# A batched matrix product: one TensorE loop over all 32 batches, the first pair of x loaded in fp32, the last pair's output copied over all partitions

## The chip, the cores and the metric

The kernel runs on one core of one Trainium2 chip. The metric is the device time of one execution in microseconds (us). The engines are TensorE (PE; its weight loads are listed apart as PEld), VectorE (DVE), ScalarE (ACT), GpSimd (POOL) and SyncE (SP). SP and POOL issue the transfers between DRAM and the on-chip memory here; these all run on the core's 16 DMA engines. TensorE writes to PSUM, and DVE and ACT copy from there to SBUF.

## The reference

```python
batch, m, k, n = 32, 512, 1024, 768
x = randn(batch, m, k)        # float32
weight = randn(batch, k, n)   # float32
out = np.matmul(x, weight).astype(np.float32)
```

There are 32 independent products of a 512x1024 matrix with a 1024x768 matrix. Inputs and output are fp32 in DRAM. x is 2.10 MB a batch, weight 3.15 MB and out 1.57 MB.

## The kernel before

**Precision and layout.** The products run in bf16. POOL's DMAs cast while they load: `load_w(b)` brings the weights of batch b into one of four slots `ws` (L92), and `load_x(k)` brings the x of two batches into one of two slots `xs` (L101). Such a pair slot holds the one batch in partitions 0 to 63 and the other in 64 to 127, eight rows of x to a partition. TensorE needs x with k on the partitions, so `transpose` (L153) turns it by multiplying with an identity: the bf16 pairs are taken as fp32 words, one 128x128 block of words in each of 32 transposes per pair, in eight groups of four. DVE copies each group from PSUM (`pts`) to `both` (`spread_pair`, L233). `multiply(b, mt)` (L134) then makes one of four row blocks of a batch: eight steps over k, each with two matmuls (512 and 256 columns) into the PSUM banks `pms`. Two blocks share three banks.

**The batches before.** Batch 0 is alone. SP loads its x in fp32 (L359) into `x_first`, which lies in an output slot; TensorE transposes fp32 numbers, and `spread_first` casts them (L216). Batches 1 to 30 go in pairs (1,2), (3,4), and so on; batch 31 is alone again, with an x load of half the size (L99) and its own `spread_last` (L236). On TensorE, `on_pe` has the code of batch 0, then a loop of seven turns (L191) with two pairs in each, then the code of one more pair and of batch 31. All other engines have their instructions written out. At the end of a turn TensorE lowers the semaphores that count the copies, so that the same constants serve in each turn.

**Outputs.** ACT and DVE copy the banks to an output slot (L265, L268, L279, L281). A slot of `outs` holds batches (0,1), (2,3) and so on, batch 2a in partitions 0 to 63 and 2a+1 in the rest, and is stored with one DMA of 3.15 MB (`store`, L109). The last two batches are copied over all 128 partitions (L276): batch 30 to a tile of its own, `one`, batch 31 to a slot of `outs`. They are stored in halves by SP (`store_half`, L115). `slot_free` waits until a slot's earlier store has landed.

**Order of the transfers.** POOL's list (`on_pool`) sets it by hand: w0, x of pair 0, w1, w2, x of pair 1, and w3 go without any wait; then, in each odd batch, the x of the pair after the next (after the transposes of two pairs earlier, `pt_done`), the store of an earlier output pair, and a w (after the products of four batches earlier, `mm_done`); in each even batch a w. Three stores (11 to 13) are kept until after the last w. SP waits for each w in turn and passes a flag to TensorE (`landed`, L307, semaphore `s_wr`); ACT does the same for x (`s_xr`). TensorE takes these flags in `take` (L157). SP then issues the half of batch 30, store(14), and the other three halves.

Of the kernel before, what the change touches and what calls it, by code (L numbers as in the profile page):

```python
# [12 lines left out]
def kernel(  # L13
# [16 lines left out]
    AHEAD = 3  # L30
    LATE = 4
    HELD = 4
    GROUPS = 2 * MT
    W_SLOTS, X_SLOTS, OUT_SLOTS = 4, 2, 4
    LOOPS = (B - 4) // W_SLOTS
    LOOPED = 2 * LOOPS

# [3 lines left out]
    x_view = x.rearrange("b (mi mo) k -> b mi mo k", mi=P)  # L41
    pair_view = x[1:B - 1].rearrange("(p r) (mi mo) k -> p (r mi) mo k", r=2, mo=2 * MT)
    out_view = out.rearrange("b (mi mo) n -> b mi (mo n)", mi=P)
# [9 lines left out]
    outs = [sbuf(f"out{i}", [P, 2 * ROW], F32) for i in range(OUT_SLOTS)]  # L53
    one = sbuf("one", [P, ROW], F32)
    x_first = outs[3][:, :MT * K].rearrange("p (mo k) -> p mo k", mo=MT)
# [11 lines left out]
    s_first, s_zero, s_ident = sem("s_first"), sem("s_zero"), sem("s_ident")  # L67
# [13 lines left out]
    def pt_done(k):  # L81
        return GROUPS * (k + 2)

    def out_done(b):
        return 2 * (b + 1)
# [8 lines left out]
    def load_x(k):  # L94
        if k >= X_SLOTS:
            pool.wait_ge(s_pt, pt_done(k - X_SLOTS))
        slot = xs[k % X_SLOTS]
        if 2 * k + 1 == B - 1:
            pool.dma_start(out=slot[:, :MT], in_=x_view[B - 1]).then_inc(s_x[k % X_SLOTS], 16)  # L99
        else:  # L100
            pool.dma_start(out=slot, in_=pair_view[k]).then_inc(s_x[k % X_SLOTS], 16)  # L101
# [5 lines left out]
    def store(eng, a, sem):  # L107
        copied(eng, out_done(2 * a + 1) - 1)
        eng.dma_start(out=two_view[a], in_=outs[a % OUT_SLOTS]).then_inc(sem, 16)  # L109

    def store_half(b, p):
        src = one if b == B - 2 else outs[(b // 2) % OUT_SLOTS]
        half = slice(p * N2, (p + 1) * N2)
        copied(sp, 2 * b + p)
        sp.dma_start(out=out_view[b, :, half], in_=src[:, half]).then_inc(s_fin, 16)  # L115
# [3 lines left out]
    def stationary(b, mt):  # L119
        if b == 0 or b == B - 1:  # L120
            return both[mt][:, 0].rearrange("p j h i r -> p j (h i) r")
        return both[mt][:, (b - 1) % 2].rearrange("p j h i r -> p j (h i) r")
# [20 lines left out]
    def rows_of(b, g):  # L143

        if b == 0:
            return [x_first[:, g // 2, JT * (g % 2) + i::KT] for i in range(JT)]
        words = xs[(b // 2) % X_SLOTS].bitcast(F32)
        mo = g if b == B - 1 else g // 2 + MT * (g % 2)
        return [words[:, mo, j::JT] for j in range(JT)]

    def transpose(b, g):
        for i, rows in enumerate(rows_of(b, g)):
            last = pe.transpose(pts[g % 2][:, i, :], rows, ident)  # L153
        last.then_inc(s_pt, 1)
# [4 lines left out]
    def pair_on_pe(k, q):  # L159

        b = 2 * k + 1
        take(s_xr)
        for g in range(GROUPS):
            if GROUPS * q + g > 1:
                pe.wait_ge(s_c, GROUPS * q + g - 1)
            transpose(b, g)
        for r in range(2):
            take(s_wr)
            for mt in range(MT):
                at = 4 * q + 2 * r + mt // 2  # L170
                if not r:
                    pe.wait_ge(s_c, GROUPS * q + 2 * mt + 2)
                pe.wait_ge(s_a, at + 1 + mt % 2)
                if b + r == B - 2 and mt == MT - 1:
                    pe.wait_ge(s_dp, 2 * (B - 2))
                else:
                    pe.wait_ge(s_d, at + 1 + mt % 2)
                multiply(b + r, mt)

    def on_pe():  # L180
        pe.wait_ge(s_ident, 1)
        pe.wait_ge(s_first, 16)
        for g in range(GROUPS):
            if g > 1:
                pe.wait_ge(s_c, g - 1)
            transpose(0, g)
        pe.wait_ge(s_c, GROUPS).then_inc(s_c, -GROUPS)
        take(s_wr)
        for mt in range(MT):
            multiply(0, mt)  # L190
        with pe.Fori(0, LOOPS):  # L191
            for q in range(2):
                pair_on_pe(q, q)
            pe.wait_ge(s_c, 2 * GROUPS).then_inc(s_c, -2 * GROUPS)
            pe.wait_ge(s_a, 9).then_inc(s_a, -8)
            pe.wait_ge(s_d, 9).then_inc(s_d, -8)
        pair_on_pe(LOOPED, 0)
        b = B - 1
        take(s_xr)
        for g in range(MT):  # L200
            pe.wait_ge(s_c, GROUPS + max(g - 1, 0))
            transpose(b, g)
        take(s_wr)
        for mt in range(MT):
            j = 2 * b + mt // 2
            pe.wait_ge(s_c, GROUPS + mt + 1)
            pe.wait_ge(s_ap if mt % 2 else s_a, j - 1 if mt % 2 else 5 + mt // 2)
            pe.wait_ge(s_dp, j - 1)
            multiply(b, mt)
# [3 lines left out]
    def spread_first(g):  # L213
        xT, pt = both[g // 2][:, 0].rearrange("p j h i r -> p j (h i) r"), pts[g % 2]
        for j in range(2):
            last = dve.tensor_copy(  # L216
                xT[:, 2 * (g % 2) + j].rearrange("p (h i) r -> p r h i", h=2),
                pt[:, 2 * j:2 * j + 2].rearrange("p r (i h) -> p r h i", h=2),
            )
        return last  # L220

    def spread_pair(k, g):

        pt = pts[g % 2].bitcast(BF16).rearrange("p j (b i r) -> p j b i r", b=2, r=2)
        tile, half = both[g // 2], g % 2
        if 2 * k + 2 == B - 2:

            rows = tile[:, 1].rearrange("p j h i r -> p j (h i r)").rearrange(
                "p j (m r) -> p j m r", r=2
            )  # L230
            dve.tensor_copy(tile[:, 0, :, half], pt[:, :, 0])  # L231
            return dve.tensor_copy(rows[:, :, half::2, :], pt[:, :, 1])  # L232
        return dve.tensor_copy(tile[:, :, :, half].rearrange("p b j i r -> p j b i r"), pt)  # L233

    def spread_last(g):
        return dve.tensor_copy(  # L236
            both[g][:, 0].rearrange("p j h i r -> p (j h i r)"),
            pts[g % 2].bitcast(BF16).rearrange("p j m -> p (j m)"),
        )

    def slot_free(eng, b):
        a = b // 2
        if a >= OUT_SLOTS and b % 2 == 0 and b < B - 2:
            eng.wait_ge(s_st[a % OUT_SLOTS], 16 * (a // OUT_SLOTS))
        if b == B - 1:
            eng.wait_ge(s_st[a % OUT_SLOTS], 16 * (a // OUT_SLOTS))

    def pieces(b, p, i):

        pm = pms[p][i]  # L250
        if b >= B - 2:
            dst = one if b == B - 2 else outs[(b // 2) % OUT_SLOTS]
            at = p * N2 + 512 * i
            return [(dst[:, at:at + 512], pm)]
        mine = outs[(b // 2) % OUT_SLOTS][H * (b % 2):H * (b % 2 + 1)]
        starts = [p * N2 + h * ROW + 512 * i for h in range(2)]
        return [(mine[:, at:at + 512], pm[H * h:H * (h + 1)]) for h, at in enumerate(starts)]

    def out_on_act(b, p):
        j = 2 * b + p  # L260
        if p == 0:
            slot_free(act, b)
# [7 lines left out]
    def out_on_dve(b, p):  # L270
        j = 2 * b + p
        if p == 0:
            slot_free(dve, b)
        dve.wait_ge(s_mm, 2 * j + 2)
        if b >= B - 2:
            dve.tensor_copy(*pieces(b, p, 1)[0]).then_inc(s_dp, 1)  # L276
            return
# [4 lines left out]

    def on_dve():

        for b in range(B):
            if b == 0 or b % 2:
                spread = {0: spread_first, B - 1: spread_last}.get(b)
                for g in range(MT if b == B - 1 else GROUPS):
                    dve.wait_ge(s_pt, (0 if b == 0 else pt_done(b // 2 - 1)) + g + 1)
                    (spread(g) if spread else spread_pair(b // 2, g)).then_inc(s_c, 1)  # L290
                if b:
                    out_on_dve(b - 1, 1)
            out_on_dve(b, 0)
            if b % 2 or b == B - 1:
                out_on_dve(b, 1)

    def on_act():
        for b in range(B):
            out_on_act(b, 0)
            if b % 2 == 0:  # L300
                landed(act, (s_x, s_xr), b // 2)
            out_on_act(b, 1)

    def landed(eng, what, i):

        slots, ready = what
        eng.wait_ge(slots[i % len(slots)], 16 * (i // len(slots) + 1)).then_inc(ready, 1)  # L307

    def on_pool():
# [12 lines left out]
        load_x(0)  # L322
        load_w(1)
        load_w(2)
        load_x(1)
        for b in range(B):
            if b % 2 and b + AHEAD + 1 < B:
                load_x((b + AHEAD) // 2)
            a = (b - 5) // 2
            if b % 2 and 0 <= a < B // 2 - 1 - HELD:  # L330
                store(pool, a, s_st[a % OUT_SLOTS])
            if b + AHEAD < B:
                load_w(b + AHEAD)
            if b == B - LATE:
                for a in range(B // 2 - 1 - HELD, B // 2 - 2):
# [60 lines left out]
```

## Time and profile before

| | us |
|---|---|
| median of 3 runs | 513.71 (513.47 to 514.14) |
| the profiled execution | 514.01 |
| its span, from the first instruction to the last | 512.2 |
| TensorE's first matmul starts at | 12.41 |
| last matmul group starts at, and takes | 490.72, 10.56 |
| last store is issued at, and lands after | 502.09, 9.0 |

| engine | busy, us | share |
|---|---|---|
| PE | 437.9 | 85% |
| DVE | 206.8 | 40% |
| ACT | 110.2 | 22% |
| POOL | 33.7 | 7% |

Busy times are those of instructions that work on data; waiting and issuing DMAs are not counted. The slices of the page cut the span into 40 parts of 12.8 us, with a digit for the busy tenths of each. The GB/s of the DMA rows and windows count what is written at the destination; a load that casts fp32 to bf16 reads twice that from DRAM. Both the span and the two times around it are needed later: the profiled execution took 1.8 us more than its span, and 0.3 us more than the median.

### The profile page before, as it was taken

What the parts mean: (1) busy time and instruction counts of PE and PEld (TensorE: products, weight loads), DVE (VectorE), ACT (ScalarE), POOL (GpSimd) and SP (SyncE); (2) the same over time, 40 slices, a digit from 0 to 9 for tenths busy, and PEclk for the clock granted to TensorE, in tenths of its full rate; (3) what the DMA queues carried; (4) which work ended last, traced back from release to release, by engine and by line L of the source; (5) the groups of instructions that cost most, each with busy time, mean ns of one, the idle gap of its engine ahead of it and who ended that gap; (6) DMA issues with size and microseconds to landing.
All of it is one profiled execution on the core that took longest, in us unless ns stands there. A gap on an engine that the chain in (4) does not pass through costs nothing. (4 is left out here: it accounts for less than half of the span.)

```text
span 512.2 us, 6109 instructions
## 1 busy us (share of the span) xinstructions
PE 437.9 (85%) x2576; PEld 278.8 (54%) x2576; DVE 206.8 (40%) x332; ACT 110.2 (22%) x189; POOL 33.7 (7%) x68
## 2 busy tenths in 40 slices
PE   0899989999795997979989798898969979799991
PEld 0666656666463654636646365464635646456660
DVE  0463543545362352533525245153631615416230
ACT  1013122222211221112221122112122121221210
POOL 3000000101010010100101001010100100100000
PEclk9999999999997998979989899799998989979997
DMA  8999999999999999999999999999999999999996
GB/s 254 214 214 222 222 207 224 213 225 325 220 335 218 240 312 224 333 218 255 297 222 337 218 264 286 219 339 218 288 266 213 341 216 306 250 214 257 432 429 290
DMA packets 9803, 135.40 MB, mean 264 GB/s; under 512 B 1088, under 2 KB 1088, under 8 KB 1600
## 3 DMA queue, kind: packets, MB, share of 16 engines
q0 software_dynamic: 8928, 126.88, 96.3%
q1 hardware_dynamic: 864, 8.39, 4.0%
q8 instruction: 5, 0.08, 0.1%
q14 instruction: 6, 0.05, 0.0%
HBM read 167.77 MB, written 50.33 MB: 426 GB/s over the span
## 5 line engine op out<-in xcount | busy, mean ns | idle before, releaser
L134 PE MATMUL pm<-w,xT 128*128 128x256 bf16 (+1 forms) x2048 | 356.2, 337 | 40.2 <-PEq L157 40.2
L134 PEld LDWEIGHTS pm<-w,xT 128*128 128x128 bf16 x2048 | 205.8, 101 | 186.2 <-issue 61.5
L279 DVE COPY out<-pm 64x512 f32<-64x512 f32 x120 | 82.5, 687 | 198.9 <-PE pm L134 198.1
L265 ACT COPY out<-pm 64x512 f32<-64x512 f32 (+1 forms) x122 | 70.7, 580 | 292.8 <-PE pm L134 292.1
L233 DVE COPY xT<-pt 128x1024 bf16<-128x1024 bf16 x112 | 72.2, 687 | 61.0 <-PE pt L153 61.0
L153 PE MATMUL pt<-ident,x 128*128 128x128 f32 x496 | 80.0, 302 | 10.5 <-DVE xT L233 9.5
L153 PEld LDWEIGHTS pt<-ident,x 128*128 128x128 f32 x496 | 69.2, 209 | 21.8 <-DVE xT L233 17.4
L268 ACT COPY out<-pm 64x512 f32<-64x512 f32 (+1 forms) x62 | 35.8, 578 | 90.0 <-PE pm L134 90.0
L281 DVE COPY out<-pm 64x512 f32<-64x512 f32 x60 | 41.2, 686 | 0.0
L101 POOL DMA_DIRECT2D x<-in_x_dram x15 | 8.0, 532 | 266.6 <-PE pt L153 266.4
L92 POOL DMA_DIRECT2D w<-in_weight_dram x32 | 17.2, 538 | 125.4 <-PE pm L134 124.4
L153 PE MATMUL pt<-ident,out 128*128 128x128 f32 x32 | 6.9, 373 | 12.7 <-DMA out<-in_x_dram 12.4
L153 PEld LDWEIGHTS pt<-ident,out 128*128 128x128 f32 x32 | 5.3, 207 | 14.1 <-issue 12.4
L216 DVE CAST xT<-pt 128x256 bf16<-128x256 f32 x16 | 6.0, 441 | 14.4 <-PE pt L153 14.1
L109 POOL DMA_DIRECT2D out_dram<-out x14 | 7.5, 536 | 1.2 <-DVE out L281 0.7
L231 DVE COPY xT<-pt 128x512 bf16<-128x512 bf16 x8 | 3.4, 420 | 4.1 <-PE pt L153 4.1
L276 DVE COPY out<-pm 128x512 f32<-128x512 f32 x2 | 1.4, 692 | 8.4 <-PE pm L134 8.4
L236 DVE COPY xT<-pt 128x1024 bf16<-128x1024 bf16 x4 | 2.6, 688 | 5.2 <-PE pt L153 5.2
L232 DVE COPY xT<-pt 128x512 bf16<-128x512 bf16 x8 | 3.3, 416 | 0.0
L276 DVE COPY one<-pm 128x512 f32<-128x512 f32 x2 | 1.4, 687 | 3.2 <-PE pm L134 3.2
L265 ACT COPY one<-pm 128x512 f32<-128x512 f32 x2 | 1.2, 585 | 4.0 <-PE pm L134 4.0
L268 ACT COPY one<-pm 128x512 f32<-128x512 f32 x2 | 1.2, 586 | 4.0 <-PE pm L134 4.0
(8 smaller groups left out, 2.7 us busy)
## 6 DMA issues: line engine op xcount, KB each, us to landing
w<-in_weight_dram POOLq DMA_DIRECT2D x32, 1536.0 KB, 41.6
out_dram<-out POOLq DMA_DIRECT2D x14, 3072.0 KB, 36.9
x<-in_x_dram POOLq DMA_DIRECT2D x15, 2048.0 KB, 30.0
out_dram<-out SPq DMA_DIRECT2D x1, 3072.0 KB, 19.9
out<-in_x_dram SPq DMA_DIRECT2D x1, 2048.0 KB, 11.3
out_dram<-one SPq DMA_DIRECT2D x2, 768.0 KB, 13.4
out_dram<-out SPq DMA_DIRECT2D x2, 768.0 KB, 10.0
x<-in_x_dram POOLq DMA_DIRECT2D x1, 1024.0 KB, 25.3
```

Of the source, the lines that this page charges most:

```text
L92: pool.dma_start(out=ws[b % W_SLOTS], in_=w_view[b]).then_inc(s_w[b % W_SLOTS], 16)
L101: pool.dma_start(out=slot, in_=pair_view[k]).then_inc(s_x[k % X_SLOTS], 16)
L109: eng.dma_start(out=two_view[a], in_=outs[a % OUT_SLOTS]).then_inc(sem, 16)
L134: last = pe.matmul(pm[bank][:, at:at + size], xT[:, ko // 2, :, ko % 2], w[:, ko, off:off + size], start=(ko == 0), stop=(ko == KT - 1),)
L153: last = pe.transpose(pts[g % 2][:, i, :], rows, ident)
L216: last = dve.tensor_copy(xT[:, 2 * (g % 2) + j].rearrange("p (h i) r -> p r h i", h=2), pt[:, 2 * j:2 * j + 2].rearrange("p r (i h) -> p r ...
L231: dve.tensor_copy(tile[:, 0, :, half], pt[:, :, 0])
L233: return dve.tensor_copy(tile[:, :, :, half].rearrange("p b j i r -> p j b i r"), pt)
L265: last = act.copy(*piece)
L268: act.copy(*pieces(b, p, 2)[0]).then_inc(s_ap, 1)
L279: last = dve.tensor_copy(*piece)
L281: dve.tensor_copy(*pieces(b, p, 2)[1]).then_inc(s_dp, 1)
```

## The change

Pairs now begin at batch 0, (0,1) to (30,31), so that the pairs of x and of the output are the same ones.

- TensorE: one loop of eight turns, two pairs in each, holds all 32 batches. Nothing stands before or after it but the wait for the identity. The closing branch is marked with a hint. Semaphores are lowered by the last wait of a turn that needs them (`await_copies`) instead of by waits of their own; ACT and DVE raise `s_a` and `s_d` by two at the start.
- The first pair's x: SP loads all of it, 4.19 MB in fp32, to the space of output slots 2 and 3. DVE casts four of its eight rows per partition into `xs[0]`, ACT the other four (`cast_first`). ACT's last cast waits for DVE's and raises `s_xr`. TensorE's transposes are the same as for every pair.
- Load order: w0, w1, x of pair 1, w2, w3; then per pair an x, a store and two w. Two stores (12, 13) are kept until after the last w instead of three.
- The last pair: batch 30 and batch 31 share one output slot, each over all 128 partitions, copied in pieces of 64 partitions each; the tile `one` is gone. `spread` makes two DVE copies a group there. SP issues store(14) ahead of the four halves.

```diff
-    LOOPS = (B - 4) // W_SLOTS
-    LOOPED = 2 * LOOPS
+    LOOPS = B // W_SLOTS
...
-    pair_view = x[1:B - 1].rearrange("(p r) (mi mo) k -> p (r mi) mo k", r=2, mo=2 * MT)
+    x_view = x.rearrange("(p r) (mi mo) k -> p (r mi) mo k", r=2, mo=2 * MT)
...
+    x_first = all_outs[:, 4 * ROW:4 * ROW + 2 * MT * K].rearrange("p (mo k) -> p mo k", mo=2 * MT)
...
     def pt_done(k):
-        return GROUPS * (k + 2)
+        return GROUPS * (k + 1)
+    def last_out(b):
+        return outs[(PAIRS - 1) % OUT_SLOTS][:, ROW * (b % 2):ROW * (b % 2 + 1)]
...
+    def await_copies(s, n, last, step):
+        wait = pe.wait_ge(s, n)
+        if n == last:
+            wait.then_inc(s, -step)
...
+    def pair_on_pe(k):
         take(s_xr)
         for g in range(GROUPS):
+            if GROUPS * k + g > 1:
+                pe.wait_ge(s_c, GROUPS * k + g - 1)
+            transpose(k, g)
+        for b in (2 * k, 2 * k + 1):
             take(s_wr)
             for mt in range(MT):
+                if b % 2 == 0:
+                    await_copies(s_c, GROUPS * k + 2 * mt + 2, 2 * GROUPS, 2 * GROUPS)
+                at = 2 * b + mt // 2 + 1 + mt % 2
+                await_copies(s_a, at, 9, 8)
+                await_copies(s_d, at, 9, 8)
+                multiply(b, mt)
     def on_pe():
         pe.wait_ge(s_ident, 1)
...
-        with pe.Fori(0, LOOPS):
-            for q in range(2):
-                pair_on_pe(q, q)
...
+        with nc.Fori(0, LOOPS, engines=[mybir.EngineType.PE], hint_back_edge=True):
+            for k in range(2):
+                pair_on_pe(k)
...
+    def spread(k, g):
         pt = pts[g % 2].bitcast(BF16).rearrange("p j (b i r) -> p j b i r", b=2, r=2)
+        if k == PAIRS - 1:
+            for b in range(2):
+                rows = both[g // 2][:, b].rearrange("p j h i r -> p j (h i r)")
+                rows = rows.rearrange("p j (m r) -> p j m r", r=2)[:, :, g % 2::2, :]
+                last = dve.tensor_copy(rows, pt[:, :, b])
+            return last
+        return dve.tensor_copy(both[g // 2][:, :, :, g % 2].rearrange("p b j i r -> p j b i r"), pt)
...
         if b >= B - 2:
-            return [(dst[:, at:at + 512], pm)]
+            return [(last_out(b)[half, at:at + 512], pm[half]) for half in rows]
...
+    def cast_first(eng, copy, rows):
+        eng.wait_ge(s_first, 16)
+        for mo in rows:
+            if mo == 2 * MT - 1:
+                eng.wait_ge(s_cast, 1)
+            last = copy(xs[0][:, mo], x_first[:, mo])
+        return last
     def on_dve():
+        dve.sem_inc(s_d, 2)
+        cast_first(dve, dve.tensor_copy, range(MT)).then_inc(s_cast, 1)
...
     def on_act():
+        act.sem_inc(s_a, 2)
+        cast_first(act, act.copy, range(MT, 2 * MT)).then_inc(s_xr, 1)
         for b in range(B):
             out_on_act(b, 0)
-            if b % 2 == 0:
-                landed(act, (s_x, s_xr), b // 2)
+            if b % 2 and b < B - 1:
+                landed(act, s_x, s_xr, b // 2 + 1, (b // 2 + 2) // 2)
             out_on_act(b, 1)
...
-        load_x(0)
         load_w(1)
+        load_x(1)
         load_w(2)
-        load_x(1)
...
+        load_w(3)
+        for k in range(PAIRS - 2):
+            load_x(k + 2)
+            if k >= 2:
+                store(pool, k - 2, s_st[(k - 2) % OUT_SLOTS])
+            load_w(2 * k + 4)
+            load_w(2 * k + 5)
+        for a in range(PAIRS - 2 - HELD, PAIRS - 2):
+            store(pool, a, s_st[a % OUT_SLOTS])
...
-        store_half(B - 2, 0)
-        store(sp, B // 2 - 2, s_fin)
-        store_half(B - 2, 1)
-        store_half(B - 1, 0)
-        store_half(B - 1, 1)
+        store(sp, PAIRS - 2, s_fin)
+        for b in (B - 2, B - 1):
+            for p in range(2):
+                store_half(b, p)
```

## The prediction

> **What bounds the kernel now.** I read the page's head, slices and byte counts first, to see which resource has no idle time.
>
> ```profile
> span 512.2 us, 6109 instructions
> ...
> PE 437.9 (85%) x2576; PEld 278.8 (54%) x2576; DVE 206.8 (40%) x332; ACT 110.2 (22%) x189; POOL 33.7 (7%) x68
> ...
> DMA  8999999999999999999999999999999999999996
> ...
> HBM read 167.77 MB, written 50.33 MB: 426 GB/s over the span
> ```
>
> The DMA row has a 9 in all slices but the first and the last; no compute engine is near that. Second, the windows by stage (the columns after the granted clock are DMA share and GB/s as written; loads halve fp32 to bf16, so 218 written is 436 read).
>
> ```profile
> 0.00:2.00 2.00, 0.00 (x0) 0.00 (x0) 0.00 (x0) 1.09 (x1) 0.73 (x5) 1.00 0.09 25
> 2.00:12.40 10.40, 0.00 (x0) 0.02 (x1) 0.00 (x0) 0.19 (x1) 3.33 (x8) 1.00 1.01 295
> 31.00:115.00 84.00, 80.06 (x499) 52.77 (x497) 41.07 (x64) 21.42 (x37) 5.28 (x10) 1.00 1.02 218
> ...
> 482.00:508.00 26.00, 18.98 (x119) 11.98 (x117) 5.26 (x8) 4.10 (x7) 0.00 (x0) 0.94 0.99 421
> 508.00:511.00 3.00, 0.00 (x0) 0.00 (x0) 0.00 (x0) 0.00 (x0) 0.00 (x0) 0.50 0.22 92
> 511.00:512.20 1.20, 0.00 (x0) 0.00 (x0) 0.00 (x0) 0.00 (x0) 0.00 (x0) 0.50 0.00 0
> ```
>
> Loads run at 436 GB/s, stores at 421. So 167.77 MB / 436 = 384.8 us and 50.33 MB / 421 = 119.5 us: 504.3 us of transfers. With 2.0 us ahead of the first one and 1.2 us after the last, 507.5 of the 512.2 us are explained. The other 4.7 us are the ramp at the start and the last 3 us, where 92 GB/s say that only a few of the 16 DMA engines are still working: they finish unevenly. Third, the waits:
>
> ```profile
> POOL x L101 <- PE pt L153: 266.4, 13, 31.4
> POOL w L92 <- PE pm L134: 124.4, 14, 9.3
> PE pm L134 <- PEq L157: 40.2, 13, 5.2
> ```
>
> TensorE waits 40.2 us for weights (L157 takes the flag that SP passes on after a landing). POOL waits for TensorE to free buffers, but that does not starve the queue: in the issue table a w takes 41.6 us from issue to landing, of which its own 3.15 MB are 7.2 us, so it stands about 34 us behind others. The timeline shows why: a pair of batches that waits for nothing takes TensorE 112.02 - 85.56 = 26.46 us (5.66 us of transposes, 20.8 of products); its transfers take 9.6 (x) + 14.4 (w) + 7.5 (out) = 31.5 us. TensorE has 5.0 us to spare in every pair.
>
> **The change part by part.** Bytes: the same 167.77 and 50.33 MB of DRAM. What moves is the *first* transfers, the order of a few, and TensorE's code.
>
> First x: SP now loads 4.19 MB in fp32 instead of 2.10, and the pool queue loads 2.10 MB less with a cast. SP still issues it first (0.95 us, first packets at 2.0), so the start of the DMA does not move. Rate bounds for the moved 2.10 MB: 389 GB/s in 4 to 6 us, where nearly all was SP's fp32, costs 2.10 x (1/389 - 1/436) = +0.6 us; no difference costs 0. The nearest steady row of fp32 transfers, 427 GB/s in 494 to 501 us, gives 2.10 x (1/427 - 1/436) = +0.1. I take +0.1.
>
> TensorE's start: now at 12.41 us. In the DMA view 80 SP packets of 16 KB and 2 of POOL's start from 1.2 to 6.0 us, so 5 on each engine; after that SP and POOL share. The remaining 48 of 128 (0.79 MB) took until 12.3 us: 125 GB/s. Afterwards 4.19 - 1.31 = 2.88 MB remain, 23 us at that rate, landing at 29; alone it would land at 2.0 + 9.6 = 11.6. Rows are now 32 KB long and SP's 24 KB rows go as one packet, so its share should grow; I take 21. Then the casts, four 128x1024 on DVE and four on ACT. The nearest rows, 128x1024 bf16 at 687 ns and 64x512 f32 at 687 (DVE) and 580 (ACT), bound DVE by 4 x 0.69 = 2.7 and 8 x 0.69 = 5.5, ACT by 8 x 0.58 = 4.6 (scaled by elements); ACT's last waits for DVE's four, so 2.7 to 5.5 + 1.2 = 6.7. I take 4.6: TensorE starts at about 26 us, between 14 and 36.
>
> Is that on the path? Only if the queue runs dry. The queue holds SP's x (9.6), w0 to w3 (28.8) and x1 (9.6) without any wait: work until 50.0 us. TensorE finds w0 and w1 there (9.6 + 14.4 us of transfers, 26 us). Then in order x2 until 59.6, w4 66.8, w5 74.0, x3 83.6, w6 90.8, w7 98.0. The tightest is w7: load_w(7) waits for batch 3's products, two pairs after the start, T0 + 52.9, + 0.5 for the issue, + at most 4.3 us to the first packet (POOL's first issue at 1.48, packets at 5.8). 90.8 - 57.7 gives T0 < 33.1. With T0 = 26, 7 us of cover remain. The others (w5 35.5, x4 34.6, x2 39.5) are looser, and from store(0) on each pair brings 31.5 us of transfers against 26.5 of compute. So the late start costs 0; without the cover it is one us per us.
>
> The DVE casts are fp32 from SBUF to SBUF. [...]
>
> One loop: prologue (32 transposes, 64 products), two pairs, and an epilogue become two pairs. A turn closes with a branch:
>
> ```profile
> L191 PEldq COMPARE_BRANCH  x7: 76/208/228, 83.2 to 459.0; - x7
> ```
>
> One branch more, plus a hint of unknown cost: between 0 and, for a missed 16 KB of code, 5.2 us (the longest idle of TensorE that the waits show) per turn. TensorE's 2 x 5.0 us of slack in a turn cover both ends. [...] The row has 0.2 us a branch, for a body of 640 instructions (320 matmuls, each with its weight load), and the instruction queue q8 fetches nothing from 80 to 460 us. [...] Code: q8 fetched 5 blocks (0.08 MB), two of them after 460; half the code needs two or three less. Each occupies one DMA engine by 16 KB, 0.6 us at 436/16 GB/s; it helps only if that engine is the last: 0 to -0.6, taken -0.1.
>
> The end: POOL keeps two stores (6.3 MB, 14.9 us) instead of three behind the last weights, SP the same five (3.15 + 4 x 0.79 MB, 14.9 us). The last store was issued at 502.09 and landed 9.0 us later, at 511.1 (issue rows). If that end holds, the last w lands near 511.1 - 29.8 = 481; then batch 31's 10.4 us (13.3 where the granted clock fell, at 448 us): products end by 492 to 495, against 501.3 now. The last pair's copies over halves of the partitions are twice as many: after the last product DVE has 3 x 0.69 = 2.1 us instead of 0.7, and SP issues the last half at about 495 to 498 instead of 502.09. At 498 the queue still has 13 us of work, 1.9 of them its own. Cover 11 us; it hid 7 us before. Cost 0. `spread` in the last pair takes 2 x 0.42 instead of 0.69 eight times, 1.2 us, under the same cover. The x of the other pairs is asked for at pt_done(k) as before, with tens of us of queue ahead of it. SP's list of weight landings is unchanged, and its stores still stand behind the last of them.
>
> Sum: 512.2 + 0.1 - 0.1 = 512.2 us of span. The profiled execution took 514.01, 1.8 around its span, and the median of the runs is 0.3 below it: 513.7 for the median afterwards.
>
> New waits: DVE and ACT wait for SP's x before anything else, and behind them stand only the spreads and copies that need TensorE's first results; ACT's last cast waits for DVE's four, priced above. ACT's wait for the next pair's landing moves from the middle of batch 2k to the middle of 2k+1; behind it are that batch's remaining copies, and TensorE at that point needs the same x. SP issues store(14) ahead of the halves of batch 30, which stand behind its wait; pair 14's copies are done a batch earlier, so that wait is none. POOL issues w1 ahead of x1, 7 us of queue in the right direction for batch 1. The last pair's copies wait in slot_free for store(11), which now stands ahead of w30 in the queue and so has landed before batch 30 can start. Each costs 0.
>
> **The rivals.** (1) Slower: the queue runs dry once, at w7 near 91 us. Place: POOL's wait in load_w. Decides from T0 = 33. For it: SP got only 125 GB/s beside POOL, and 29 + 6.7 = 36; price 36 - 33.1 = 3 us, 517. Against: the long rows, and a first-packet delay of 4.3 us that falls in the busy start. (2) Slower: the hint makes each closing branch fetch a block, 7 x 0.6 = 4.2 us on one engine; if that one is among the last, 516 to 518. Against: q8 is silent in the loop now. (3) Faster: the uneven finish shrinks, since less code is fetched late and the products end some 6 us earlier. Half of the 3 us at 92 GB/s: 512.2. Against: the stores were never waited for at the end. (4) The change does not do what it says: the hint does nothing visible; that is my forecast's time.
>
> **How the numbers follow.** Forecast (no idle DMA, same bytes): 0.70, with its own range 512.8 to 514.6. Rival 1: 0.08, rival 2: 0.06, something slower that no row shows: 0.04; rival 3: 0.12. A measurement of this kernel can tell about 0.2%, 1.0 us, from no change. So slower 0.18, faster 0.12. The range 512.5 to 515.6 takes in the unpriced ends (+0.6, -0.6 and the runs' own 0.7 us) and the near parts of rivals 1 and 3.
>
> **What would show it.** Right: DMA digits of 9 throughout, 426 GB/s, TensorE's first transposes at 22 to 30 us, its waits at the landing flag still there (5 us a pair, less early on), last product near 493, the last store issued over 8 us before the end. Wrong: a slice with a lower DMA share between 50 and 120 us (rival 1), more than 5 packets on q8 (rival 2), a last stretch shorter than 2 us (rival 3), or total DMA rate below 424 GB/s without any gap.

## The result and the profile after

The changed kernel takes 514.36 us (median, 513.72 to 515.04), the kernel before 513.38 on the same chip (512.94 to 514.14): a ratio of 1.0017, 95% interval 1.0011 to 1.0024. It is slower by 1.0 us. The 513.71 us of the front page was a high reading of the kernel before, and so was its profiled execution (514.01): in the five comparisons of this document its median was 513.34 to 513.63. Ratios below are against the kernel before in the same comparison, "+0.98" is the difference of those medians.

The page of the changed kernel (an execution of 514.2 us):

```profile
span 512.4 us, 6044 instructions
...
PE 429.7 (84%) x2512; PEld 277.5 (54%) x2560; DVE 212.9 (42%) x332; ACT 116.4 (23%) x197; POOL 33.2 (6%) x67
...
DMA  8999999999999999999999999999999999999996
...
q8 instruction: 1, 0.02, 0.0%
HBM read 167.77 MB, written 50.33 MB: 426 GB/s over the span
```

The row of 9s, the bytes and the 426 GB/s are those of before. TensorE's work is off the path as before, and what the change moved lies where the prediction put it. Three answers show it: TensorE's waits (us in total, times, longest), the casts of the first pair (busy, mean ns, idle before), and the last rows of the timeline:

```profile
PE pm L125 <- PEq L143: 26.7, 8, 5.3
PE pt L139 <- PEq L143: 22.8, 1, 22.8
```

```profile
L231 DVE CAST x<-outs 128x1024 bf16<-128x1024 f32 x4 | 2.5, 689 | 18.7 <-DMA outs<-in_x_dram 18.7
L231 ACT CAST x<-outs 128x1024 bf16<-128x1024 f32 x4 | 3.9, 1042 | 16.5 <-DMA outs<-in_x_dram 16.5
```

```profile
497.78 1.39 DVE L221 COPY outs<-pm 64x512 f32<-64x512 f32 x2 [3.20 <-PE pm L125]
499.09 0.69 DVE L223 COPY outs<-pm 64x512 f32<-64x512 f32 x1
499.85 0.33 SPq L108 DMA_DIRECT2D out_dram<-outs  x1
```

SP's x lands at 18.7 us, TensorE starts at 22.8, still waits for weights at the landing flag (L143), and the last half-store is issued at 499.85, 11.4 us ahead of its landing. None of these places shows a stall of the queue.

That leaves the start, the finish and what lies around the span, and it is in the last two. The last microseconds, DMA share and GB/s in the last two columns; first the kernel before in the run b_again (513.43 us), which is nearer to its median than the profile of the front page, then the changed kernel:

```profile
507.00:508.00 1.00, 0.00 (x0) 0.00 (x0) 0.00 (x0) 0.00 (x0) 0.00 (x0) 0.50 0.74 307
508.00:509.00 1.00, 0.00 (x0) 0.00 (x0) 0.00 (x0) 0.00 (x0) 0.00 (x0) 0.50 0.37 154
509.00:510.00 1.00, 0.00 (x0) 0.00 (x0) 0.00 (x0) 0.00 (x0) 0.00 (x0) 0.50 0.18 74
510.00:511.00 1.00, 0.00 (x0) 0.00 (x0) 0.00 (x0) 0.00 (x0) 0.00 (x0) 0.50 0.00 0
```

```profile
507.00:508.00 1.00, 0.00 (x0) 0.00 (x0) 0.00 (x0) 0.00 (x0) 0.00 (x0) 0.50 0.78 326
508.00:509.00 1.00, 0.00 (x0) 0.00 (x0) 0.00 (x0) 0.00 (x0) 0.00 (x0) 0.50 0.21 86
509.00:510.00 1.00, 0.00 (x0) 0.00 (x0) 0.00 (x0) 0.00 (x0) 0.00 (x0) 0.50 0.18 74
510.00:511.00 1.00, 0.00 (x0) 0.00 (x0) 0.00 (x0) 0.00 (x0) 0.00 (x0) 0.50 0.10 43
```

At 507 us both have about the same left to do: 307 + 154 + 74 = 535 KB before, 326 + 86 + 74 + 43 = 529 KB after. Shared evenly by 16 engines it would be done near 508.3 in both. From 508 us on the changed kernel has it on fewer engines (DMA share 0.21 against 0.37), so the last one is later. The landings in the trace say the same; a store has 16 of them (1072 landings for the 67 issues of the changed kernel), taken here as one for each engine. Of the last sixteen the first comes at 508.0 us in each profile, the last 2.5 us later in b_again, 3.1 in the first profile of before, 3.3 in the changed kernel, and the span ends 1.1 us after the last. Their mean hardly moves: 508.87, 509.09 and 508.94 us. So the mean engine lost no more, at the start or later, than two executions of the same kernel differ. How far the last landing lies behind this mean, 1.65, 2.00 and 2.35 us in these three, is called the **lag of the slowest engine** below. One profile is one execution, and the two of the kernel before differ too: the first has 609 KB left at 507 us.

Over all timed runs the median span is 512.4 us after, and 511.5 to 511.8 before in each of the four comparisons with experiments: 0.6 to 0.9 us of the loss are inside the span. What lies around it grew from 1.80 us to 1.92 (means of time less span), another 0.12.

### The profile page after: what moved, and what is told of

Same layout as the page of the kernel before. It is cut to its first block, busy times and chain, and to the rows that moved or that the text cites. A ratio compares the mean times of both kernels' runs of the same rounds, so it can differ in the third digit from the quotient of the medians.

```text
span 512.4 us, 6044 instructions
## 1 busy us (share of the span) xinstructions
PE 429.7 (84%) x2512; PEld 277.5 (54%) x2560; DVE 212.9 (42%) x332; ACT 116.4 (23%) x197; POOL 33.2 (6%) x67
## 2 busy tenths in 40 slices
DMA packets 9655, 136.38 MB, mean 266 GB/s; under 512 B 1072, under 2 KB 1072, under 8 KB 1584
## 5 line engine op out<-in xcount | busy, mean ns | idle before, releaser
L125 PE MATMUL pm<-w,xT 128*128 128x256 bf16 (+1 forms) x2000 | 348.6, 334 | 35.0 <-PEq L143 26.7
L221 DVE COPY outs<-pm 64x512 f32<-64x512 f32 x128 | 88.1, 688 | 198.5 <-PE pm L125 197.1
L210 ACT COPY outs<-pm 64x512 f32<-64x512 f32 x128 | 74.2, 580 | 272.9 <-PE pm L125 272.1
L139 PE MATMUL pt<-ident,x 128*128 128x128 f32 x512 | 84.5, 308 | 33.1 <-PEq L143 22.8
L187 DVE COPY xT<-pt 128x1024 bf16<-128x1024 bf16 x120 | 77.7, 687 | 65.5 <-PE pt L139 65.5
L139 PEld LDWEIGHTS pt<-ident,x 128*128 128x128 f32 x512 | 72.6, 209 | 45.3 <-issue 22.7
L213 ACT COPY outs<-pm 64x512 f32<-64x512 f32 x64 | 37.0, 578 | 91.6 <-PE pm L125 91.6
L223 DVE COPY outs<-pm 64x512 f32<-64x512 f32 x64 | 43.9, 686 | 0.0
L231 DVE CAST x<-outs 128x1024 bf16<-128x1024 f32 x4 | 2.5, 689 | 18.7 <-DMA outs<-in_x_dram 18.7
L103 POOL DMA_DIRECT2D out_dram<-outs x14 | 7.5, 536 | 7.8 <-DVE outs L223 7.6
L231 ACT CAST x<-outs 128x1024 bf16<-128x1024 f32 x4 | 3.9, 1042 | 16.5 <-DMA outs<-in_x_dram 16.5
```

The costliest lines, as they stand in the source:

```text
L125: last = pe.matmul(pm[bank][:, at:at + size], xT[:, ko // 2, :, ko % 2], w[:, ko, off:off + size], start=(ko == 0), stop=(ko == KT - 1),)
L139: last = pe.transpose(pts[g % 2][:, j, :], words[:, mo, j::JT], ident)
L187: return dve.tensor_copy(both[g // 2][:, :, :, g % 2].rearrange("p b j i r -> p j b i r"), pt)
L210: last = act.copy(*piece)
L213: act.copy(*pieces(b, p, 2)[0]).then_inc(s_ap, 1)
L221: last = dve.tensor_copy(*piece)
```

## The experiments

**The same kernel again.** b_again is the kernel before, unchanged.

> The kernel before, unchanged, to see how far its own executions differ and to have a second profile of it. If the 22 runs are typical, it is the same as before (ratio 1.000, within 0.1%), and its span is nearer 511.6 us than the 512.2 of the first profile: 513.4 (median of 22 runs) less the 1.8 us around the span. If the span is 512.2 again, the 1.0 us by which the change is slower lies outside the profiled span.

513.37 us, ratio 0.9998 (0.9989 to 1.0007). A 0.1% difference can be seen here, not much less.

**The first x.** a_halfx loads half of the first pair's x with POOL, cast by the DMA.

```diff
-        sp.dma_start(x_first, x_view[0]).then_inc(s_first, 16)
+        sp.dma_start(x_first, x_view[0][:, :MT]).then_inc(s_first, 16)
+        pool.dma_start(out=xs[0][:, MT:], in_=x_view[0][:, MT:]).then_inc(s_x[0], 16)
-    cast_first(dve, ..., range(MT)); cast_first(act, ..., range(MT, 2 * MT))
+    cast_first(dve, ..., range(MT // 2)); cast_first(act, ..., range(MT // 2, MT))
```

> The changed kernel with half of the first pair's x (four of eight rows in each partition) loaded by POOL with a cast, as much fp32 by SP as in the kernel before (2.10 MB). Theory X (the fp32 load of the first pair costs the 1.0 us: 2.10 MB more at a lower rate): back to 513.4 to 513.6, ratio 1.000. Theory E (the order of the last stores) and theory L (the loop, its hint, its code): stays at 514.3, ratio 1.0017.

514.69 us, 1.0026 (1.0016 to 1.0036), +1.35. Fewer bytes in fp32 and half the casts bring nothing; TensorE started at 21.7 us, little earlier. The load's type isn't the cause.

**The hint.** In a_nohint the loop is a plain one; in b_hint the kernel before gets the hint on its seven turns.

```diff
-        with nc.Fori(0, LOOPS, engines=[mybir.EngineType.PE], hint_back_edge=True):
+        with pe.Fori(0, LOOPS):
```

> The changed kernel without the hint on the closing branch. Theory L in its form 'the hint costs': back to 513.4. Theories X and E: 514.3. TensorE has 10 us of slack in a turn, so a slower branch should not show; whether a block of code is fetched after the span, as in the changed kernel (16 KB at 513.1 us), shows whether the hint causes it.

> The kernel before with the hint alone on its loop of seven turns. Without the hint the changed kernel took 513.83 instead of 514.36. Theory L (the hint itself costs about 0.5 us): 513.9 here, ratio 1.001. Theory U (the time is set by how unevenly the 16 DMA engines finish, and anything that shifts the engines' stalls moves it by some tenths; the hint is one of many): 513.4, ratio 1.000 within 0.1%.

a_nohint: 513.83 us, 1.0010 (1.0001 to 1.0019), +0.49, half of the +0.98, but the two intervals overlap. b_hint: 513.77, 1.0002 (0.9993 to 1.0011), +0.25, not told from no change. In the trace the hint is an instruction of its own, once a turn, and the closing branch does not get shorter by it (median 208 ns in a_nohint). The changed kernel:

```profile
L171 PEldq BRANCH_PREFETCH_HINT  x8: 31/31/45, 3.0 to 432.8; - x8
L171 PEldq COMPARE_BRANCH  x8: 88/223/249, 74.3 to 494.8; - x8
```

The instruction queue in the whole span of a_nohint:

```profile
q8 instruction: 2, 0.03, 0.0%
```

With the hint one block is fetched within the span (at 41.7 us), without it two (at 41.6 and 62.9); in neither is a block fetched in the turns after that. In the kernel before, too, the hint moves a block: b_again fetches one at 78.8 us, b_hint none there and one more at 462.0. In four of the ten profiles of kernels that have the hint on the one loop, a block comes after the span's end, as here in the changed kernel between 512.5 and 515 us, and never without the hint:

```profile
DMA packets 1, 0.02 MB, mean 7 GB/s; under 512 B 0, under 2 KB 0, under 8 KB 0
...
q8 instruction: 1, 0.02, 3.1%
```

The time around the span differs as well: 1.79 to 1.82 us on average in every kernel without the hint on the one loop, and at most 1.87 in any run; 1.83 to 2.01 in those with it, and up to 2.94 in a run. But the late block doesn't explain this: the four profiled executions that have it took 1.77 to 2.15 us around their spans, the six without it 1.78 to 2.07.

**The end.** a_endold gives batch 30 a tile of its own again, keeps three stores and issues SP's in the old order; a_nohint_endold takes the hint away too.

```diff
+    one = sbuf("one", [P, ROW], F32)
-    HELD = 2
+    HELD = 3
-        store(sp, PAIRS - 2, s_fin)
-        for b in (B - 2, B - 1): ...
+        store_half(B - 2, 0)
+        store(sp, PAIRS - 2, s_fin)
+        store_half(B - 2, 1) ...
```

> The changed kernel with the end in the old order: batch 30 goes to a tile of its own, three stores (11 to 13) are kept until after the last weights, and SP issues the first half of batch 30 ahead of store(14). Theory E (two kept stores and SP's five make the DMA engines finish less evenly): back to 513.4. Theories X and L: 514.3.

> The changed kernel without the hint and with the old end (a tile of its own for batch 30, three kept stores, SP's old order). What remains of the change is the pairing from batch 0 and the first pair's load. If hint and end make up the 1.0 us (0.5 and 0.2 by the two single runs): 513.6. Theory U, with the pairing as its main cause: 513.8 to 514.2.

a_endold: 514.19 us, 1.0015 (1.0006 to 1.0024), +0.85. a_nohint_endold: 514.10, 1.0010 (1.0001 to 1.0019), +0.58. The end isn't the cause: undoing it brings 0.13 with the hint and costs 0.09 without.

**Where engines fall apart.** The packet records show two kinds of event by which engines fall behind the others: one of them also fetches the 16 KB of code (0.94 us for that packet, so about +1 us on one engine at 41.7), and single packets of the load that stands just ahead of a store take 0.1 to 1.3 us longer. In the changed kernels the largest group of such packets comes ahead of the first store, x of pair 4 at 106.7 to 108.8 us; in b_again it is small there, and the largest comes at 177 us. By the 16 landings of each load the lag of the slowest engine collects over the whole run: in the changed kernel it is 0.3 us at 18 to 37 us, ahead of the fetch, 1.3 at 44 to 60, 1.8 at 110 to 140 and 2.6 at 455 to 482; in b_again 1.0, 0.8 and 2.0, in the first profile of before 0.9, 0.7 and 2.4. a_storefirst puts each store ahead of the x; a_storesplit cuts stores in two with the x between, so that loads change to stores twice as often.

```diff
-            load_x(k + 2)
-            if k >= 2:
-                store(pool, k - 2, s_st[(k - 2) % OUT_SLOTS])
+            if k >= 2:
+                store(pool, k - 2, s_st[(k - 2) % OUT_SLOTS])
+            load_x(k + 2)
```

```diff
+            if k >= 2: store_part(k - 2, 0)
             load_x(k + 2)
-            if k >= 2: store(pool, k - 2, ...)
+            if k >= 2: store_part(k - 2, 1)
```

> The changed kernel with each pair's store queued ahead of the x load and not behind it (store, x, w, w). The trace shows packets of x prolonged by 0.1 to 1.0 us just where the queue goes over from x to a store, first at 106 to 109 us, and engines that are late become later there. Theory T (the change from x to a store is what unsettles the engines): the last engines finish less late, 513.4 to 513.9, and those long packets are gone or shorter. If any change from loads to a store does it: 514.3 with the long packets now among w's.

> The changed kernel with every store of POOL cut in two halves of 1.57 MB, one ahead of the x load and one behind it: twice as many changes between loads and stores. Theory T (each change costs the late engines some tenths): the last engine later by up to twice as much, 514.8 to 516. If the unevenness has another source: 514.3.

a_storefirst: 514.74 us, 1.0024 (1.0015 to 1.0034), +1.22; the long packets are now those of the w ahead of the first store, at 98 to 99 us. So they do not belong to x. a_storesplit: 514.62, 1.0019 (1.0010 to 1.0028), +1.10: twice as many changes cost 0.12 more, within the error. The number of changes doesn't set the loss.

**The start of TensorE.** b_late0 delays TensorE in the kernel before; a_early brings it forward in the changed one; a_early_noh_eo and a_early_noh are a_early without the hint, the first with the old end too.

```diff
         pe.wait_ge(s_first, 16)
+        pe.wait_ge(s_x[0], 16)
```

```diff
-        sp.dma_start(x_first, x_view[0]).then_inc(s_first, 16)
+        sp.dma_start(x_first[:, :MT], x_view[0][:, :MT]).then_inc(s_first, 16)
+        sp.dma_start(x_first[:, MT:], x_view[0][:, MT:]).then_inc(s_half, 16)
...
         eng.wait_ge(s_first, 16)
+        eng.wait_ge(s_half, 16)
...
     def on_pool():
-        load_w(0)
         pool.memset(ident, 0.0).then_inc(s_zero, 1)
...
+        pool.wait_ge(s_first, 16)
+        load_w(0)
         load_w(1)
```

> The kernel before, with one added wait: TensorE starts its first transposes only when the pool queue's first pair load has landed too, at about 23 us instead of 12.4. Nothing else is changed; the queue holds work until 50 us either way. Theory P (phase): in the changed kernel the long packets come already at the first store because all of POOL's issues from 60 us on fall about 11 us later against the transfers. Then this kernel shows the long packets at its own first store, near 112 us, the first-to-last difference of the last store's landing grows from 2.5 to over 3 us, and the median is 0.4 to 1.0 us above that of the kernel before. Rival L (layout): it is the pairing of the batches (addresses of x against out, first load), not the phase. Then this kernel takes the time of the kernel before within 0.3 us, with its large step near 177 us as before.

> The changed kernel, with SP's first x load cut into two of four rows each, and POOL's first load issued only when the first of these has landed, so that SP's x does not share the engines: x is to land near 12 us instead of 18.7 and TensorE to start near 16 instead of 22.8 us. Theory P: POOL's issues come 6 us earlier against the transfers, the large step at 106 to 109 us shrinks or moves, and the median falls by 0.4 to 0.8 us from that of the changed kernel (514.4), unless POOL's first packets come after SP's last (a gap of up to 2 us, which then adds fully and shows as a lower DMA share before 14 us). Rival L: the step stays at 106 to 109 us and the time at 514.2 to 514.6.

> As the kernel before it in this list, without the hint and with the end as in the kernel before (batch 30 in a tile of its own, three stores kept, SP's order of stores). What remains of the change is the pairing from batch 0 with its first load. Theory P: 513.3 to 513.7, no longer to be told from the kernel before. Rival L: 514.0 to 514.3, as with the late start (514.10).

> The changed kernel with the earlier start (x of the first pair alone on the engines) and without the hint, with its own end. If the hint costs 0.3 to 0.5 and the sharing at the start 0.2, and these add: 513.6 to 513.9, not to be told from the kernel before. If the old end was what helped in the kernel with both undone: 514.0 to 514.3.

b_late0: 515.41 us, 1.0040 (1.0026 to 1.0054), +2.0. It did not test what it was meant to: TensorE started at 26.0 us, and in this kernel the x of pair 4 waits for later transposes than in the changed one, so the queue ran nearly dry: it is issued 77.8 us after TensorE's start, against 60.4 in the changed kernel. POOL's issue (start first) and the windows around it:

```profile
103.82 0.53 POOL L101 DMA_DIRECT2D x<-in_x_dram  x1 [15.54 <-PE pt L153]
```

```profile
100.00:104.00 4.00, 3.63 (x24) 2.91 (x24) 3.52 (x6) 0.00 (x0) 0.18 (x1) 1.00 1.03 218
104.00:106.00 2.00, 2.00 (x15) 1.21 (x13) 1.99 (x4) 0.00 (x0) 1.40 (x3) 1.00 1.14 190
106.00:108.00 2.00, 2.00 (x15) 1.22 (x13) 0.15 (x1) 1.16 (x2) 0.00 (x0) 1.00 0.76 147
108.00:112.00 4.00, 4.00 (x27) 2.44 (x26) 1.99 (x3) 1.21 (x3) 0.00 (x0) 1.00 1.00 209
112.00:114.00 2.00, 2.00 (x14) 1.12 (x13) 0.04 (x1) 0.57 (x2) 0.00 (x0) 1.00 1.39 213
114.00:116.00 2.00, 2.00 (x14) 1.23 (x13) 1.94 (x3) 0.53 (x1) 0.53 (x1) 1.00 0.89 123
```

Against 218 GB/s the five windows from 104 on lack 56 + 142 + 36 + 10 + 190 = 434 KB, 2.0 us: the whole loss. Of this, 198 KB are missing between 104 and 108 us, just behind the late issue: there the queue shows as slower packets, not as a hole. Another 200 KB are missing between 112 and 116, when a store and a w had long been issued behind the x (at 104.39 and 104.91); these are the long packets ahead of the first store: beside the usual 1.23 us of such a packet they took 22.8 us too long in sum, 1.4 us for each of the 16 engines, more than in any other run (7.7 and 0.5 in the changed kernel). Why is not shown. The DMA digits stay at 9 all the same.

a_early: 514.16 us, 1.0017 (1.0008 to 1.0026), +0.75. x landed at 14.0 us, and TensorE started at 19.4, not at 16: ACT's table load of 1.28 us, which stood at 0.98 us in the changed kernel and here comes behind the first wait, at 14.11, lay between the landing and its 3.9 us of casts. The long packets stay at 107 to 109 us, so earlier issues by POOL do not move them. a_early_noh_eo: 513.75, 1.0007 (0.9998 to 1.0016), +0.34. a_early_noh: 513.80, 1.0003 (0.9994 to 1.0012), +0.17. With the hint gone and the first x alone on the engines, the changed kernel can't be told from the kernel before; the new end may stay.

**The bound of the late start.** TensorE of the changed kernel waits in addition for w1 (a_t29) or the second pair's x (a_t38).

```diff
         pe.wait_ge(s_ident, 1)
+        pe.wait_ge(s_w[1], 16)     # a_t29
+        pe.wait_ge(s_x[1], 16)     # a_t38, in its place
```

> The changed kernel; TensorE waits in addition for the landing of batch 1's weights, so it starts near 28 us instead of 22.8. w7 is then issued near 83 us for a turn in the queue at 92. Theory C (cover, as the prediction has it): below a start of 33 us it costs nothing; 514.2 to 514.6, no lower DMA share, and the late start is no part of the 1.0 us. Rival G (graded): a later start costs before the queue is dry, as 3.3 us earlier brought 0.2 us; then 5 us more give 514.7 to 515.2.

> The same, but TensorE waits for the landing of pair 1's x, so it starts near 38 us, 5 us past the bound of 33.1 that the prediction gave for w7. By its working (T0 + 52.9 + 0.5 + at most 4.3 us to the first packet) w7 comes some 4.5 us late, one us per us: 517.5 to 519, with a lower DMA share near 92 to 97 us. If the first packet comes after 1.3 us, as for x4 in the kernel before with the late start (issued at 103.8, first packets at 105.1), the bound is 36 and the cost 1 to 3 us: 515.5 to 517.5. Theory G gives 515 to 516 and no dip.

a_t29 (start at 28.2): 514.75 us, 1.0022 (1.0013 to 1.0031), +1.12 against +0.98: within each other's intervals, and no dip. a_t38 (start at 37.9): 516.89 us, 1.0061 (1.0047 to 1.0074), +3.26. The dip is where the prediction's first rival put it, at w7:

```profile
92.79 0.53 POOL L90 DMA_DIRECT2D w<-in_weight_dram  x1 [9.87 <-PE pm L125]
```

```profile
90.00:92.00 2.00, 1.95 (x12) 1.17 (x12) 0.00 (x0) 1.08 (x2) 0.00 (x0) 1.00 1.10 233
92.00:94.00 2.00, 1.70 (x13) 1.47 (x12) 1.00 (x2) 0.58 (x1) 0.53 (x1) 1.00 0.48 98
94.00:96.00 2.00, 1.81 (x13) 1.54 (x13) 1.57 (x3) 0.00 (x0) 0.00 (x0) 1.00 1.15 184
96.00:98.00 2.00, 1.82 (x14) 1.57 (x14) 1.70 (x3) 0.00 (x0) 0.00 (x0) 1.00 0.93 197
```

These lack (240 + 68 + 42) KB / 218 = 1.6 us. Most of the rest of the 2.3 us over the changed kernel lies, as in b_late0, in the long packets ahead of the first store, at 108 to 113 us: 17.9 us in sum, 1.1 us an engine, 0.6 more than in the changed kernel.

**Later stores, other addresses.** a_late issues each of POOL's stores one pair later; a_reverse takes the pairs in reverse order, so that all DRAM addresses differ.

```diff
-            if k >= 2:
-                store(pool, k - 2, s_st[(k - 2) % OUT_SLOTS])
+            if k >= 3:
+                store(pool, k - 3, s_st[(k - 3) % OUT_SLOTS])
-    HELD = 2
+    HELD = 3
```

```diff
+    def turned(b):
+        return 2 * (PAIRS - 1 - b // 2) + b % 2
-        ... in_=w_view[b] ... in_=x_view[k] ... out=two_view[a] ...
+        ... in_=w_view[turned(b)] ... in_=x_view[PAIRS - 1 - k] ... out=two_view[PAIRS - 1 - a] ...
```

> The changed kernel with all of POOL's stores one pair later in the queue (the first one after the x of pair 5, three kept behind the last weights). The first change from loads to stores then lies near 138 us. Theory P: what counts is how far POOL's issues are ahead of the transfers at the first store; with one pair more of loads ahead of it, the queue is 31.5 us less deep at that point and the step is as large or larger, at 135 to 140 us: 514.2 to 514.8. Rival L or a step that belongs to every first store: also at its first store, same time. A rival F (fetch): the 1.0 us on one engine from the fetch at 41.7 us alone sets the end; then the step at the first store makes no difference and all of these stay at 514.4. If the step vanishes, the time falls to 513.6 to 514.0.

> The changed kernel with the pairs taken in the reverse order (pair p in the code is pair 15 - p in DRAM), so that all DRAM addresses differ at every point of time and all else is the same. If the long packets at 106 to 109 us, ahead of the first store, hang on the addresses, they move or vanish and the time moves by 0.3 us or more; if not, they stay at 106 to 109 us and the time at 514.2 to 514.6.

a_late: 515.55 us, 1.0043 (1.0030 to 1.0057), +2.14. It made a new wait: output slots are free too late, and the copies wait for stores to land,

```profile
ACT outs L210 <- DMA out_dram<-outs: 160.2, 11, 16.7
```

so TensorE's last product comes late and the queue stands nearly still from 506 to 508 us (DMA shares 0.27 and 0.21). The long packets moved with the first store, to 131 to 133 us. a_reverse: 514.73 us, 1.0025 (1.0014 to 1.0037), +1.10, long packets again at 107 to 109. They do not hang on the addresses.

## Why the prediction was wrong

Its bound, its covers and its places held. No slice of the DMA row is below 9 but the first and the last, and the mean landing does not move; the late start up to 28 us is hidden but for some tenths at most; the rest of the moved work costs nothing that a run shows. TensorE started at 22.8 us (forecast 26: x landed at 18.7 instead of 21, and ACT's four casts, the longer side, took 3.9 us where 4.6 were taken). The products ended at 497.7 instead of 492 to 495 and the last store was issued at 499.85 instead of 495 to 498. The working put one batch behind the last weights; two stood behind the last wait for weights:

```profile
475.10 3.27 PE L125 MATMUL pm<-w,xT 128*128 128x512 bf16 x10 [3.18 <-PEq L143]
```

From 475.10 on batches 30 and 31 ran back to back for 22.6 us. The 11 us of cover are there all the same. The bound of 33.1 us for the start was a little strict: in a_t38 w7 was issued 54.9 us after the start, its first packets followed by 1.3 us, not 0.5 + 4.3, and the packets of w6 ahead of it ended near 93, not 90.8, so the bound is about 36 to 37; on its two sides lie 28.2 us (nothing that can be told) and 37.9 (2.3 us more than the changed kernel). Rival 1 had the right mechanism and place and did not occur.

**The step that failed** is the term of 4.7 us for the ramp and the uneven finish, with the 1.8 us around the span, which the sum took over from one execution and changed by -0.1 for less code. Measured, the span grew by 0.6 to 0.9 and what lies around it by 0.12; of the 4.7 us it is the finish that grew. The sum costed every edit by whether the queue runs dry. That is the right question for the mean of the 16 engines, and its answer was right: the mean of the last landings stays. The time, however, is set by the slowest engine, and for its lag there was no row in the sum but the one for code.

The other kernels say the same. In the fifteen profiles whose queue did not run dry (all but b_late0, a_t38 and a_late) the mean of the last sixteen landings lies between 508.75 and 509.31 us, with the kernel before (508.87 to 509.09) in the midst of the others. The slowest engine lags behind it by 1.65 to 2.04 us in the three profiles of the kernel before (one of them b_hint), by 2.22 to 2.29 in the four of changed kernels without the hint, and by 2.02 to 3.11 in the eight with it.

That the forecast of 513.7 came within 0.7 us of 514.36 is luck: the high reading that it started from hid a third of the loss.

What of it comes from which part, as far as the runs tell:

| kernel | hint | over the kernel before, us | median span |
|---|---|---|---|
| the change | yes | +0.98 | 512.4 |
| a_early | yes | +0.75 | 512.3 |
| a_endold | yes | +0.85 | 512.3 |
| a_storesplit, a_reverse, a_t29 | yes | +1.10, +1.10, +1.12 | 512.8, 512.8, 512.7 |
| a_storefirst, a_halfx | yes | +1.22, +1.35 | 512.8, 512.9 |
| a_nohint, a_nohint_endold | no | +0.49, +0.58 | 512.0, 512.3 |
| a_early_noh_eo, a_early_noh | no | +0.34, +0.17 | 512.0, 512.0 |
| the kernel before with the hint | yes | +0.25 | 512.0 |

**The hint**: the eight kernels with it on the one loop whose queue did not run dry lie at +0.75 to +1.35, the four without at +0.17 to +0.58. Pair by pair, taking it away brought 0.49 (the change), 0.27 (old end) and 0.58 (early start), and adding it to the kernel before cost 0.25; the mean is 0.4, with an error of about 0.3 either way (estimated from the intervals of the seven kernels). In the three pairs with one loop about 0.1 of it lies around the span, in b_hint nothing. No single pair is separated by its intervals, except that the change (1.0011 to 1.0024) and a_early_noh (0.9994 to 1.0012) hardly meet. The prediction's second rival had this part and its sign, but not its way: not a block in each turn (q8 has fewer packets, not more). In the steady turns no fetch is shown, with or without the hint: q8 moves nothing from 80 to 460 us in the kernel before, and within the span nothing after 41.7 us in the changed kernel and after 62.9 in a_nohint.

**The first pair's load and start**: 0.2 to 0.3 (a_early against the change, a_early_noh against a_nohint, both in the same direction, neither separated); later starts go the same way, +0.75, +0.98, +1.12 for 19.4, 22.8 and 28.2 us, but a_halfx, which starts at 21.7, does not (+1.35). **The end**: undoing it moved the time by -0.13, +0.09 and +0.17, nothing. The rest, +0.17 in a_early_noh, is within the error.

**Open**: how the hint makes the slowest engine later, and why the load ahead of the first store has longer packets in the changed kernels (2.8 to 10.2 us in sum where that load is an x and the queue is not nearly dry, against 0 to 2.1 in the kernel before). Excluded as reasons for the latter are x itself (a_storefirst), the addresses (a_reverse), the hint (a_early_noh) and the end (a_endold). POOL's issue is not too late for them either: that x is issued 13 us ahead of its first packet in b_again, 17 in the changed kernel and 20 in a_early. Only where it is nearly late, in b_late0 and a_t38, are the sums larger. They are still 6.6 us in a_early_noh (7.7 in the changed kernel), which is not measurably slower than the kernel before, so they cannot be the main cause of the loss.

No version was faster than the kernel before.

## What to carry to other kernels

Where the DMA queue is the bound and never idle, cost an edit twice: for the mean of the DMA engines (bytes, a dry queue) and for the slowest of them; put the second in the sum as an unknown of some tenths of a microsecond, above nothing more than below it (here +0.17 to +1.35 us for the versions of the changed kernel whose queue did not run dry). Compare the windows of the last microseconds: equal bytes left with a longer tail mean an uneven finish, not more work (here 535 KB before and 529 after at 507 us, the last landing 2.5 and 3.3 us behind the first of its sixteen). And take the base from several executions: here the one profile shown was 0.6 us above the kernel's median, more than half of what was to be predicted.

## What was not expected of the hardware

- The branch hint, which removes one fetch of 16 KB at 63 us, goes with a longer time: 0.4 us on average over four pairs, give or take 0.3. On the one loop the time around the span then reaches up to 2.94 us, where no run without it is above 1.87; four of its ten profiles show a block fetched after the span, but these are not the longer ones.
- A pool-queue load issued when the queue was nearly dry had its first packets 1.3 us after the issue (103.82 to 105.1 and 92.79 to 94.0), where POOL's first load of all needed 4.3 (1.48 to 5.8 in the kernel before); but its first packets then took up to 1.1 us longer each. In the first of these cases 198 KB, 0.9 us, were lost within 4 us of the issue without a digit below 9 in the DMA row.
- The 16 DMA engines drift apart over a run whose queue is never idle: the slowest is 1.0 to 1.3 us behind their mean at 44 to 60 us in b_again and the changed kernel, and 2.0 to 2.6 us at 455 to 482.
